# Loading and turning A for the first two regions of a 4096-cube matmul: pieces, order of issue and turns

## The chip, the cores and the metric

One core of one Trainium2 chip. The metric is device microseconds of one execution; the median of the fast runs is quoted (an execution can fall into a slower state of the chip). "Faster" or "slower" needs 2%, which is 36 us here.

## The reference

```
x = a @ b                                  # a, b: 4096 x 4096, fp32
out = where(x > 0, x, 0.01 * x)            # leaky ReLU, fp32
```

## The kernel before: the parts that matter

The product is cut into regions of 512 rows by 1024 columns: 4 row tiles (`MT`) times 2 column tiles (`NP`) of 128x512, which fill all eight PSUM banks. Chunks of k are 128 long; 32 chunks x 8 outputs = 256 matmuls to a region. Loads by POOL cast fp32 to bf16 on the way; A is then transposed on DVE.

The first two regions (the upper and the lower 512 rows, h = 0 and 1, of the same columns) share their B and are run interleaved, because loading is what is short at the start (in the kernel before, the windows view shows the DMA engines busy throughout from 5 to 140 us). The 32 chunks are cut into five segments, and a "turn" is a list of segments that are summed in PSUM for h = 0, then for h = 1. After each turn the sum is added to `part` in SBUF:

```
SEGS = [(0, 0, 4), (0, 4, 4), (1, 0, 8), (2, 0, 8), (3, 0, 8)]   # unit, first chunk, chunks
TURNS = [[0], [1], [2, 3, 4]]
...
def load_a(mb, h, s, mt, tiles):                 # loads and transposes in one
    ...
    a16 = a16_pool.tile([P, 4 * tiles, kw // 4], BF16, name="a16")
    for q in range(4):
        nc.gpsimd.dma_start(a16[32 * q:32 * q + 32], src.rearrange("(g i) w -> i g w", i=32))
    nc.vector.transpose(dst ..., a16 ...)
...
def spill(t, h, mt, banks):
    for nt in range(NP):
        kept = part[h][:, mt, nt * NT:(nt + 1) * NT]
        if t == 0: ...                            # ACT or DVE copies
        else:
            nc.vector.tensor_add(kept, banks[mt, nt], kept)
...
for quarter in range(4):                          # inside one step
    if last:
        todo = [(quarter, c) for c in range(kc)]
    else:
        todo = [(mt, quarter * kc // 4 + c) for c in range(kc // 4) for mt in range(MT)]
    ...                                           # matmuls of todo
    if last:
        spill(t, h, quarter, banks)
    quarter_of(following, quarter)                # a quarter of the next step's loads and transposes
```

A "step" is one segment for one h. Steps 0 to 3 have 32 matmuls each, steps 4 to 9 have 64.

## Time and profile before

| kernel before | us |
|---|---|
| time, median of 3 runs | 1792.63 |
| profiled span | 1790.5 |

The prediction below splits the span into the stream of real matmuls, the end of the kernel and the rest. The rest, the start of TensorE and its waits before 89 us, is about 20.6 us, and all a change of the start can win is part of it. The lines that show where it sits stand in the prediction. The word **lag** is used throughout as defined there: the time at which a matmul starts, less 0.2156 us for every real matmul before it. A wait raises it, nothing lowers it, and two kernels compare by their last lag.

### The profile page before, as it was taken

To read this page: it belongs to the slowest core of one execution; us is meant where nothing else is said; L and a number is where in the kernel's file an instruction comes from. 1 tells how busy PE (TensorE), PEld (TensorE's weight loads), DVE (VectorE), ACT (ScalarE), POOL (GpSimd) and SP (SyncE) were. 2 spreads that over 40 slices of the span, in tenths; PEclk is the share of its full clock that TensorE was granted. 3 is DMA by queue.
4 is the path that set the end of the run, shared out by engine and by line. 5 is a ranking of instruction groups with operands and counts; after the bars stand their busy time and mean duration, and the time that the engine had idled before them with its cause. 6 is when DMAs were issued, how large, how long until landed. Compare 5 with 4: busy or idle time off the path is not lost.

```text
span 1790.5 us, 18113 instructions
## 1 busy us (share of the span) xinstructions
PE 1775.6 (99%) x8220; PEld 803.6 (45%) x8220; DVE 141.9 (8%) x114; ACT 150.1 (8%) x266; POOL 369.0 (21%) x671
## 2 busy tenths in 40 slices
PE   8999999999999999999999999999999999999999
PEld 3444444444444444444444444444444444444444
DVE  5420000022100000002200000000220000000000
ACT  2000000000000000000000000000000000000001
POOL 5540110343002021043300202014320120201000
PEclk9999999999999999999999999999999999999999
DMA  9994661997229166398703917539860481835511
GB/s 214 215 230 94 127 144 58 190 122 128 66 71 193 53 112 135 85 187 129 129 37 94 188 47 118 117 95 201 129 116 24 106 176 48 160 75 119 117 48 47
DMA packets 163612, 212.49 MB, mean 119 GB/s; under 512 B 43600, under 2 KB 92752, under 8 KB 163536
## 3 DMA queue, kind: packets, MB, share of 16 engines
q0 software_dynamic: 143232, 141.08, 49.7%
q10 hardware_dynamic: 17856, 65.02, 9.3%
q1 hardware_dynamic: 2448, 5.24, 0.8%
q8 instruction: 64, 1.05, 0.2%
q14 instruction: 12, 0.10, 0.0%
HBM read 285.21 MB, written 67.11 MB: 197 GB/s over the span
## 4 chain that ended last, share of the span: by engine, by line
PE 95%; DMA 4%; POOL 0%; issue 0%; DVE 0%; ACT 0%; SPq 0%; DVEq 0%
PE ps L139 95%; DMA bt<-in_b_dram 2%; DMA a<-in_a_dram 1%; DMA a_in<-in_a_dram 0%; POOL a L113 0%; DVE at L114 0%; POOL bt L129 0%; ACT bt L247 0%; DVE part L216 0%; ACT o L336 0%; ACT at L254 0%; DVE a_rounded L249 0%; PE turned L252 0%; SPq L239 0%; SPq L237 0%
## 5 line engine op out<-in xcount | busy, mean ns | idle before, releaser
L139 PE MATMUL ps<-bt,at 128*128 128x512 bf16 x8192 | 1769.9, 379 | 9.2 <-DVE at L114 8.1
L139 PEld LDWEIGHTS <-at 128*128 128x128 bf16 x8192 | 801.0, 98 | 976.7 <-DVE at L114 10.0
L129 POOL DMA_DIRECT2D bt<-in_b_dram x412 | 219.7, 539 | 1099.7 <-PE ps L139 1042.0
L336 ACT ACTIVATE o<-ps 128x512 f32<-128x512 f32 x240 | 130.7, 595 | 1524.5 <-PE ps L139 1450.7
L114 DVE STREAM_TRANSPOSE at<-a 128x1024 uint32<-128x1024 uint32 x63 | 113.0, 1828 | 1165.9 <-DMA a<-in_a_dram 607.8
L113 POOL DMA_DIRECT2D a<-in_a_dram x252 | 148.5, 596 | 190.4 <-DVE at L114 125.4
L216 DVE TENSOR_TENSOR part<-ps,part 128x512 f32<-128x512 f32 x32 | 20.4, 682 | 30.9 <-PE ps L139 30.9
L219 ACT ACTIVATE o<-part 128x1024 f32<-128x1024 f32 x8 | 8.5, 1057 | 98.9 <-DVE part L216 86.8
L212 DVE COPY part<-ps 128x512 f32<-128x512 f32 x8 | 5.1, 672 | 1.7 <-PE ps L139 1.7
L214 ACT COPY part<-ps 128x512 f32<-128x512 f32 x8 | 4.4, 593 | 8.5 <-PE ps L139 5.3
L84 PE MATMUL ps<-w 128*128 128x512 bf16 x8 | 3.6, 628 | 1.2 <-DVE x L80 1.2
L247 ACT CAST bt<-b_in 128x1024 bf16<-128x1024 f32 (+1 forms) x4 | 3.8, 938 | 0.0
L252 PE MATMUL turned<-ident,a_rounded 128*128 128x128 bf16 x16 | 1.9, 246 | 0.8 <-DVE a_rounded L249 0.8
L252 PEld LDWEIGHTS <-a_rounded 128*128 128x128 bf16 x16 | 1.2, 123 | 2.7 <-DVE a_rounded L249 2.6
L84 PEld LDWEIGHTS <-w 128*128 128x128 bf16 x8 | 1.0, 138 | 2.9 <-issue 1.7
L254 ACT COPY at<-turned 128x256 bf16<-128x256 bf16 x4 | 1.8, 444 | 4.6 <-PE turned L252 4.6
L254 DVE COPY at<-turned 128x256 bf16<-128x256 bf16 x4 | 1.8, 448 | 4.4 <-ACT at L254 4.4
L249 DVE CAST a_rounded<-a_in 128x512 bf16<-128x512 f32 x4 | 1.7, 426 | 3.0 <-DMA a_in<-in_a_dram 2.7
L271 POOL CAST x<-bt 128x1 f32<-128x1 bf16 x1 | 0.2, 187 | 7.3 <-ACT bt L247 7.3
L81 ACT ACT_TABLE_LOAD x1 | 1.3, 1283 | 0.7 <-PEq L358 0.7
L267 PE MATMUL ps<-w 128*128 128x512 bf16 x4 | 1.3, 456 | 0.0
L267 PEld LDWEIGHTS <-w 128*128 128x128 bf16 x4 | 0.5, 135 | 0.4 <-issue 0.3
(10 smaller groups left out, 1.9 us busy)
## 6 DMA issues: line engine op xcount, KB each, us to landing
bt<-in_b_dram POOLq DMA_DIRECT2D x412, 256.0 KB, 7.6
out_dram<-o ACTq DMA_DIRECT2D x124, 512.0 KB, 3.3
a<-in_a_dram POOLq DMA_DIRECT2D x252, 128.0 KB, 5.6
out_dram<-o SPq DMA_DIRECT2D x8, 256.0 KB, 2.0
b_in<-in_b_dram SPq DMA_DIRECT2D x3, 512.0 KB, 5.4
a_in<-in_a_dram SPq DMA_DIRECT2D x4, 256.0 KB, 5.1
b_in<-in_b_dram SPq DMA_DIRECT2D x2, 256.0 KB, 6.6
```

Of the source, the lines that this page charges most:

```text
L84: nc.tensor.matmul(wp, w[:, :P], w, start=True, stop=True)
L113: nc.gpsimd.dma_start(a16[32 * q:32 * q + 32], src.rearrange("(g i) w -> i g w", i=32))
L114: nc.vector.transpose(dst.rearrange("p c m e -> p c (m e)").bitcast(U32) .rearrange("p c (g i) -> p g c i", g=4 * tiles), a16.rearrange("p ...
L129: nc.gpsimd.dma_start(new_b(pi, u)[:, c0 + c, :], b_rows(n, s, c))
L139: nc.tensor.matmul(ps, at[mb, h, u][:, c // 2, mt * P:(mt + 1) * P, c % 2], bt[pi, u][:, c, nt * NT:(nt + 1) * NT], start=first, stop=last,)
L212: nc.vector.tensor_copy(kept, banks[mt, nt])
L214: nc.scalar.copy(kept, banks[mt, nt])
L216: nc.vector.tensor_add(kept, banks[mt, nt], kept)
L219: nc.scalar.activation(o, part[h][:, mt, :], LRELU, alpha=alpha)
L247: copy(b0[:, i, columns(half)], b_in[:, i, columns(half)])
L254: copy(a0[:, c, i * P:(i + 1) * P, :].rearrange("p m e -> p e m"), turned[i][:, 2 * c:2 * c + 2, :],)
L336: nc.scalar.activation(o[:, cols], banks[mt, nt], LRELU, alpha=alpha)
```

## The change

Its intent: the first A of the lower half comes in two pieces so that work can start on the first; POOL's loads are released at the first B chunk instead of the second; a load and its transpose become two calls, so that all loads of the next step are issued at once at the beginning of a step, while the transposes are placed among the additions on DVE; and segments 2 and 3 are run for both halves before segment 4. The order of the very first loads changes too. (In the code, `fetch()` is the load and `turn()` the transpose; it has nothing to do with the turns of `TURNS`.)

```
-TURNS = [[0], [1], [2, 3, 4]]
+TURNS = [[0], [1], [2, 3], [4]]
...
+        def fetch(): ...        # the four DMAs
+        def turn(): ...         # the transpose
+        return fetch, turn
...
+        made = pieces_a(0, h, s, 2 if i == 1 else None) if i else []
...
-    order = []
-    for i in range(MT):
-        order += [("a", i, None)] + [("b", i, half) for half in ((0, 1) if i == MT - 1 else (None,))]
+    order = [("a", 0), ("a", 1), ("b", 0), ("a", 2), ("b", 1), ("a", 3), ("b", 2), ("b", 3)]
...
-        if (what, i) == ("b", 1):
-            nc.gpsimd.tensor_copy(x[:, :1], b0[:, 1, :1])      # POOL waits here before its first load
+        if (what, i) == ("b", 0):
+            nc.gpsimd.tensor_copy(x[:, :1], b0[:, 0, :1])
...
+        head = 0 if h else kc // 2 if last else kc
+        groups = [([(mt, c) for c in range(head) for mt in range(MT)], None)]
+        groups += [([(mt, c) for c in range(head, kc)], mt if last else None) for mt in range(MT)]
+        where = [2] if len(following) == 1 else [0, 3]         # (shortened)
...
+            for fetch in fetches[i + 1]:
+                fetch()
...
+            for piece, turn in enumerate(following):
+                if where[piece] == g:
+                    turn()
+            if leaves is not None:
+                spill(t, h, leaves, banks)
```

More of the change, by code (lines that the diff above doesn't have):

```diff
@@ L107, in load_a, with fetch, turn @@
         k0, kw = k_of(s)
-        dst = new_a(mb, h, u)[:, c0 // 2:(c0 + kc) // 2, mt * P:(mt + tiles) * P, :]
         row = ((mb * HALVES + h) * MT + mt) * P
-        a16 = a16_pool.tile([P, 4 * tiles, kw // 4], BF16, name="a16")
-        for q in range(4):
-            src = a[row:row + tiles * P, k0 + q * kw // 4:k0 + (q + 1) * kw // 4]
-            nc.gpsimd.dma_start(a16[32 * q:32 * q + 32], src.rearrange("(g i) w -> i g w", i=32))
-        nc.vector.transpose(
-            dst.rearrange("p c m e -> p c (m e)").bitcast(U32)
-            .rearrange("p c (g i) -> p g c i", g=4 * tiles),
-            a16.rearrange("p g w -> p (g w)").bitcast(U32)
-            .rearrange("p (g j c) -> p g c j", g=4 * tiles, c=kc // 2),
-        )
+        held = []
+        def fetch():
+            a16 = a16_pool.tile([P, 4 * tiles, kw // 4], BF16, name="a16")
+            for q in range(4):
+                src = a[row:row + tiles * P, k0 + q * kw // 4:k0 + (q + 1) * kw // 4]
+                to = a16[32 * q:32 * q + 32]
+                nc.gpsimd.dma_start(to, src.rearrange("(g i) w -> i g w", i=32))
+            held.append(a16)
+        def turn():
+            dst = new_a(mb, h, u)[:, c0 // 2:(c0 + kc) // 2, mt * P:(mt + tiles) * P, :]
+            nc.vector.transpose(
+                dst.rearrange("p c m e -> p c (m e)").bitcast(U32)
+                .rearrange("p c (g i) -> p g c i", g=4 * tiles),
+                held[0].rearrange("p g w -> p (g w)").bitcast(U32)
+                .rearrange("p (g j c) -> p g c j", g=4 * tiles, c=kc // 2),
+            )
+        return fetch, turn
     def b_rows(n, s, c):
@@ L129, in load_b, with pieces_a @@
         nc.gpsimd.dma_start(new_b(pi, u)[:, c0 + c, :], b_rows(n, s, c))
-    def pieces_a(mb, h, s):
-        tiles = 2 * KC // SEGS[s][2]
-        return [lambda mt=mt: load_a(mb, h, s, mt, tiles) for mt in range(0, MT, tiles)]
+    def pieces_a(mb, h, s, tiles=None):
+        tiles = tiles or 2 * KC // SEGS[s][2]
+        return [load_a(mb, h, s, mt, tiles) for mt in range(0, MT, tiles)]
     def pieces_b(pi, s):
@@ L181 @@
                     at_slot = first * KU + h * KU + u - 2 * KU + 1
-                    loads.setdefault(at_slot, []).extend(pieces_a(mb, h, s))
+                    for fetch, turn in pieces_a(mb, h, s):
+                        loads.setdefault(at_slot, []).extend([fetch, turn])
     def quarter_of(pieces, quarter):
@@ L194 @@
     ]
-    def step_loads(h, s):
-        made = pieces_a(0, h, s)
-        if h == 0:
-            own = pieces_b(0, s)
-            made = made[:1] + own[:4] + made[1:] + own[4:]
-        return made
-    queue = [step_loads(h, s) for _, h, s, _, _ in steps]
+    fetches = []
+    turns = []
+    for i, (_, h, s, _, _) in enumerate(steps):
+        made = pieces_a(0, h, s, 2 if i == 1 else None) if i else []
+        fetches.append([fetch for fetch, _ in made] + (pieces_b(0, s) if i and h == 0 else []))
+        turns.append([turn for _, turn in made])
     part = {}
@@ L227, with columns @@
     a_rounded = a16_pool.tile([P, MT, kw0], BF16, name="a_rounded", tag="a16")
-    order = []
-    for i in range(MT):
-        order += [("a", i, None)] + [("b", i, half) for half in ((0, 1) if i == MT - 1 else (None,))]
-    def columns(half):
-        return slice(0, RN) if half is None else slice(half * NT, (half + 1) * NT)
-    for what, i, half in order:
+    order = [("a", 0), ("a", 1), ("b", 0), ("a", 2), ("b", 1), ("a", 3), ("b", 2), ("b", 3)]
+    def columns(nt):
+        return slice(nt * NT, (nt + 1) * NT)
+    for what, i in order:
         if what == "a":
             nc.sync.dma_start(a_in[:, i, :], a[i * P:(i + 1) * P, :kw0])
-        else:
-            nc.sync.dma_start(b_in[:, i, columns(half)], b_rows(pairs[0], 0, i)[:, columns(half)])
+        elif i < kc0 - 1:
+            nc.sync.dma_start(b_in[:, i, :], b_rows(pairs[0], 0, i))
+        else:
+            for nt in range(NP):
+                nc.sync.dma_start(b_in[:, i, columns(nt)], b_rows(pairs[0], 0, i)[:, columns(nt)])
     a0 = new_a(0, 0, 0)
@@ L242, with take @@
     turned = [psum_pool.tile([P, kc0, P], BF16, name="turned", tag="ps") for _ in range(MT)]
-    def take(what, i, half):
+    def take(what, i):
         if what == "b":
-            copy = nc.vector.tensor_copy if half == 1 else nc.scalar.copy
-            copy(b0[:, i, columns(half)], b_in[:, i, columns(half)])
+            for nt, copy in ((0, nc.scalar.copy), (1, nc.vector.tensor_copy)):
+                copy(b0[:, i, columns(nt)], b_in[:, i, columns(nt)])
             return
@@ L259 @@
     there = {"a": [], "b": []}
-    ready = []
+    waiting = []
     begun = set()
     banks = {}
-    for n, (what, i, half) in enumerate(order):
-        take(what, i, half)
-        if n == 0:
+    for n, (what, i) in enumerate(order):
+        take(what, i)
+        if n == 1:
             for _ in range(4):
@@ L268 @@
             banks = new_banks()
-        if (what, i) == ("b", 1):
-            nc.gpsimd.tensor_copy(x[:, :1], b0[:, 1, :1])
+        if (what, i) == ("b", 0):
+            nc.gpsimd.tensor_copy(x[:, :1], b0[:, 0, :1])
             part[0] = part_pool.tile([P, MT, RN], FP32, name="part", tag="part")
-        if half != 1:
-            there[what].append(i)
-        if what == "a":
-            now = [(i, c, nt) for c in there["b"] for nt in range(NP)]
-        else:
-            now = [(mt, i, nt) for mt in there["a"] for nt in (range(NP) if half is None else (half,))]
-        ready.append(now)
-        for mt, c, nt in ready[n - 1] if n else []:
-            mm(banks[mt, nt], 0, 0, 0, 0, mt, nt, c, (mt, nt) not in begun,
-               what == "b" and half == 1 and c == kc0 - 1)
-            begun.add((mt, nt))
-    following = list(queue[1])
-    following.pop(0)()
-    for mt, c, nt in ready[-1]:
-        mm(banks[mt, nt], 0, 0, 0, 0, mt, nt, c, False, True)
+        for mt, c in waiting:
+            for nt in range(NP):
+                mm(banks[mt, nt], 0, 0, 0, 0, mt, nt, c, (mt, nt) not in begun, False)
+                begun.add((mt, nt))
+        there[what].append(i)
+        waiting = [(i, c) for c in there["b"]] if what == "a" else [(mt, i) for mt in there["a"]]
+    for fetch in fetches[1]:
+        fetch()
+    turns[1][0]()
+    for nt in range(NP):
+        for mt, c in waiting:
+            mm(banks[mt, nt], 0, 0, 0, 0, mt, nt, c, False, True)
+    for mt in range(MT):
         spill(0, 0, mt, banks)
-    for piece in following + queue[2]:
-        piece()
+    turns[1][1]()
+    for fetch in fetches[2]:
+        fetch()
     for i in range(1, len(steps)):
@@ L294 @@
         u, c0, kc = SEGS[s]
-        following = queue[i + 1] if 2 <= i and i + 1 < len(steps) else []
-        own = 2 * KU - 2 + i - (len(steps) - 2)
+        head = 0 if h else kc // 2 if last else kc
+        groups = [([(mt, c) for c in range(head) for mt in range(MT)], None)]
+        groups += [([(mt, c) for c in range(head, kc)], mt if last else None) for mt in range(MT)]
+        following = turns[i + 1] if i + 1 < len(steps) else []
+        if len(following) == 1:
+            where = [2]
+        else:
+            where = [0, 3]
+        own = 2 * KU - 2 + i - (len(steps) - 2)
+        own = list(loads.get(own, [])) if own >= 2 * KU - 2 else []
+        if i > 1 and i + 1 < len(steps):
+            for fetch in fetches[i + 1]:
+                fetch()
+        for piece in own:
+            piece()
         if first:
@@ L300 @@
                 part[h] = part_pool.tile([P, MT, RN], FP32, name="part", tag="part")
-        for quarter in range(4):
-            if last:
-                todo = [(quarter, c) for c in range(kc)]
-            else:
-                todo = [(mt, quarter * kc // 4 + c) for c in range(kc // 4) for mt in range(MT)]
+        for g, (todo, leaves) in enumerate(groups):
             for mt, c in todo:
@@ L309 @@
                        last and c == kc - 1)
-            if last:
-                spill(t, h, quarter, banks)
-            quarter_of(following, quarter)
-            if own >= 2 * KU - 2:
-                quarter_of(loads.get(own, []), quarter)
+            for piece, turn in enumerate(following):
[3 more added lines that the diff above has]
+                spill(t, h, leaves, banks)
     for r in range(HALVES, len(regions)):
```

## The prediction

> **What bounds the kernel now.** I read the page first, for which engine fills the span.
>
> ```profile
> PE 1775.6 (99%) x8220; PEld 803.6 (45%) x8220; DVE 141.9 (8%) x114; ACT 150.1 (8%) x266; POOL 369.0 (21%) x671
> ...
> PE   8999999999999999999999999999999999999999
> ```
>
> TensorE (PE) is busy nearly everywhere; only the first of the 40 slices (45 us each) is below 9. The windows view gives 1855 matmuls in each undisturbed 400 us, so one 128x512 matmul starts every 400/1855 = 0.2156 us, and the 8192 real ones need 8192 x 0.2156 = 1766.2 us. The profiled span is 1790.5. So only 24.3 us are not the matmul stream, and a change that removes no matmul can win at most those. The last matmul ends at about 1786.8 in the timeline, so 3.7 us are the last eviction and store, which the change does not touch. The rest is the start. I then asked who made PE wait in the whole trace.
>
> ```profile
> PE ps L139 <- DVE at L114: 8.1, 4, 2.4
> ...
> PE ps L139 <- DMA bt<-in_b_dram: 0.8, 1, 0.8
> PE ps L139 <- DVE part L216: 0.2, 1, 0.2
> ```
>
> The columns are total us, times, longest. Four waits for a transpose of A (L114) make up nearly all. PE's timeline says when they fall.
>
> ```profile
> 6.97 1.31 PE L139 MATMUL ps<-bt,at 128*128 128x512 bf16 x4
> ...
> 17.43 13.99 PE L139 MATMUL ps<-bt,at 128*128 128x512 bf16 x64 [2.07 <-DVE at L114]
> 33.81 7.95 PE L139 MATMUL ps<-bt,at 128*128 128x512 bf16 x36 [2.39 <-DVE at L114]
> 43.15 0.94 PE L139 MATMUL ps<-bt,at 128*128 128x512 bf16 x3 [1.40 <-DVE at L114]
> 44.31 29.30 PE L139 MATMUL ps<-bt,at 128*128 128x512 bf16 x135 [0.22 <-DVE part L216]
> 74.40 11.81 PE L139 MATMUL ps<-bt,at 128*128 128x512 bf16 x54 [0.79 <-DMA bt<-in_b_dram]
> 88.42 6.87 PE L139 MATMUL ps<-bt,at 128*128 128x512 bf16 x31 [2.20 <-DVE at L114]
> ```
>
> The reader is to see that nothing waits after 88.42. I keep one book, the **lag**: the time at which a matmul starts, less 0.2156 us for each real matmul before it. At 6.97 it is 7.0; at 17.43 (32 before it) 10.5; at 33.81 (96) 13.1; at 44.31 (135) 15.2; at 74.40 (270) 16.2; at 88.42 (324) 18.6. What the change makes of the time is what it makes of this last lag. VectorE (DVE) is 8% busy overall, but in the stretch before 44 us it is not idle at all where it matters.
>
> ```profile
> 31.31 1.29 DVE L216 TENSOR_TENSOR part<-ps,part 128x512 f32<-128x512 f32 x2 [0.44 <-PE ps L139]
> 32.52 1.23 DVE L114 STREAM_TRANSPOSE at<-a 128x1024 uint32<-128x1024 uint32 x1
> 35.60 1.29 DVE L216 TENSOR_TENSOR part<-ps,part 128x512 f32<-128x512 f32 x2 [1.85 <-PE ps L139]
> 36.81 2.02 DVE L114 STREAM_TRANSPOSE at<-a 128x1024 uint32<-128x1024 uint32 x1
> 38.75 2.44 DVE L216 TENSOR_TENSOR part<-ps,part 128x512 f32<-128x512 f32 x4
> 41.12 1.98 DVE L114 STREAM_TRANSPOSE at<-a 128x1024 uint32<-128x1024 uint32 x1
> 43.01 1.25 DVE L216 TENSOR_TENSOR part<-ps,part 128x512 f32<-128x512 f32 x2
> ```
>
> The transpose at 32.52 comes after all eight additions of the step before it, and PE, which had run dry at 31.4, starts at 33.81 when it is done. **This is an order of work on one engine, not missing data.**
>
> **What the Trainium skill says.** "TensorE: Matmul & The Clock Gate", Part 1 ("Wait — 56ns, not 53.3ns?"), gives 215.7 ns from start to start for a warm matmul of 512 columns; the trace agrees with 215.6. "PSUM — Partial Sum Buffer", "PSUM: the matmul accumulator", has eight banks, each of 512 fp32 columns, and one matmul output within one bank: a step of 4 x 2 outputs therefore fills all eight, and the next step enters a bank only once its sum is taken away. The trace shows that wait once (0.2 us, for L216). "Perfetto Trace Analysis", "Tensor Engine Instruction", calls DVE strict FIFO, so the program's order of additions and transposes is what runs; the DVE rows above stand in program order. "DMA: Bandwidth & Descriptors", "Anatomy of one DMA", fits 2.0 us + bytes/436e3, or 2.3 us as an estimate for 128 KB. The trace differs: 7.2 us median to landing for the A loads of the first 110 us, because up to eight are in flight at about 200 GB/s. The measurement decides.
>
> **The change part by part.** Steps: 0 and 1 are segment 0 of k (4 chunks, 32 matmuls, 6.9 us) for the upper and the lower half of rows; 2 and 3 the same for segment 1; then segments 2, 3, 4 (64 matmuls, 13.8 us each).
>
> *Step 0, reordered loads.* Now both A tiles come before the first B chunk, and each B chunk is rounded in halves on ACT and DVE. I worked the chain through with the trace's 0.43 (DVE rounding), 0.41 (PE transpose), 0.44 and 0.45 (ACT and DVE copies), about 0.6 and 0.45 (half chunks), and the landings it shows (first A 3.86, 1 MB by 6.2, then about 2.6 us a MB). The second A is rounded at 6.1, B chunk 0 on ACT 7.35 to 7.95, the third A from 8.2, first real matmuls at about 8.95 (before: 6.97), last A transposed at 11.2, and 26 matmuls after it: step 0 ends at about 16.75, against 15.36 before (10.88 + 4.48). Cost **+1.4**. "Loads begun at the first B chunk" moves POOL's first load from 8.75 to about 8.3 only.
>
> *Step 1, A in two pieces.* Before, four DMAs of 128 KB, issued 8.75 to 11.4, were transposed at 16.13 to 17.38. The first piece is now four of 64 KB, issued about 8.3 to 11, and should land near 14; its transpose takes half of 1.25, some 0.65 us. It is ready before 16.75, and banks are freed as step 1 needs them. The 2.07 us wait goes: step 1 starts at 16.75 instead of 17.43, lag 9.9 against 10.5. Second piece: transposed about 19, needed at 16.75 + 3.45 = 20.2.
>
> *Steps 2 to 4, transposes placed among the additions.* Step 2 starts at 23.65. It runs two chunks for all rows, then finishes row tile by row tile, so its first sum is ready after 20 matmuls at 27.95. From there I add up DVE in its new order. Before, from 26.13 to 44.26 is 18.13 us, of which 0.44 x 3 + 1.85 = 3.17 idle: 14.96 us for 16 additions and three transposes. The work is the same after. The new order is two additions, the transpose for step 3 (27.95 + 1.29 + 1.2 = 30.45, just when PE needs it at 30.55), six additions, transpose, four additions, transpose, four additions. It need not idle, so it ends at 27.95 + 14.96 = 42.9. Step 3 runs without a wait and ends at 37.45. But step 4 goes chunk by chunk over all four row tiles, and its eighth matmul needs the bank that the last of those additions frees. So the 2.39 wait goes and **a new one of about 4.5 us in total takes its place** at the start of step 4. Resume at 42.9 with 135 matmuls done: 42.9 - 29.1 = 13.8, against 15.2.
>
> *Four turns instead of three.* Segments 2 and 3 now run for both halves before segment 4. Before, the third 2 MB of B were needed from about 72 us (B wait at 74.40); now two 13.8 us steps that need only 1 MB of A come between, so loads at 200 GB/s get 27.6 us of slack. The 0.79 and the wait for a transpose queued late (2.20 at 88.42) should go, 3.4 us of lag from 15.2 to 18.6 with the small change. Added: 16 more additions, 16 x 0.65 = 10.4 us of DVE, in two steps of 13.8 us each, where the windows show DVE less than half busy; they lie beside PE.
>
> *Sum.* Final lag 13.8 against 18.6, or **-4.8 us**; by parts -0.6 by the start of step 1 (+1.4 and -2.07, rounded), -0.8 by step 4 (13.8 - 9.9 = 3.9 lost there, against 15.2 - 10.5 = 4.7) and -3.4 later. I allow 0.2 for a small new wait: 1792.6 - 4.6 = **1788.0 us**.
>
> **The rivals.** (1) DVE does not bind steps 3 and 4: if additions and transposes fit, the lag stays at 9.9 and the time is near 1784. Against: 14.96 us of DVE work in 9.5 us of PE time (27.95 to 37.45). (2) Loading is the bound: 64 KB DMAs cost POOL nearly the same issue time as larger ones (0.58 against 0.54 us for a different shape), eight instead of four come first, and segment 1's data arrive later; then the wait moves to step 2 and 2 to 4 us return, near 1791. For: the DMA share is over 1 from 10 us on. Against: 2.0 MB are due by 24 us and the rate before gave about 2.3. (3) Step 0 is worse than I have it, or PE's idle patches slow its clock: up to +2, near 1790; or its extra 1.4 us disappears in slack, near 1787. (4) The start is hidden by something later: no wait in the trace after 88.42 speaks for it, so what the start wins, the end keeps.
>
> **Range and chances.** The floor of all this is 1766.2 + 3.7 + about 9 of lag, and the 2.1 us by which the reported time exceeds the span, near 1781; returning to 1792 would need every gain spent in new waits. Eight in ten: 1785.8 to 1790.8. A change by 2% is 36 us, more than the whole start can give; only a blunder with all loads late would reach it upward. Faster 0.003, same 0.99, slower 0.007.
>
> **What would show it.** In the changed profile: first real matmul near 9, step 1 starting near 16.7 without a transpose wait; a wait of 4 to 5 us between 37 and 43 put down to additions (part) and a transpose, with DVE solid from 28 to 43; no wait for B near 74 and none near 88; steady 1855 matmuls per 400 us after. Wrong if step 2 waits for B, if step 0 ends after 18, if DVE has gaps at 28 to 43, or if a wait appears where segment 4 starts (about 97).

## The result

Median 1789.94 us in four runs (1787.88 to 1790.84) against 1793.04 in four of the kernel before. The ratio is 0.9981 (0.9963 to 0.9998). A ratio here is formed from the fast runs of both kernels in the same rounds, so it is not quite the ratio of the medians. The time was in the stated range, 1.9 us above the forecast; the forecast gain was 4.6 us, and the medians show 3.1.

PE's waits in the changed kernel (total us, times, longest):

```profile
PE ps L148 <- DVE part L225: 2.7, 4, 2.1
PE turned L262 <- DVE a_rounded L259: 1.6, 2, 1.3
PE ps L84 <- DVE x L80: 1.2, 1, 1.2
PE ps L148 <- DVE at L121: 0.9, 1, 0.9
```

L148, L225 and L121 are what L139, L216 and L114 were. The transposes, which held PE for 8.1 us, now hold it for 0.9; the additions have taken a part of their place, and the wait for B is gone. PE's timeline (start, duration, and in brackets the idle time before):

```profile
9.23 1.63 PE L148 MATMUL ps<-bt,at 128*128 128x512 bf16 x6
11.18 0.41 PE L262 MATMUL turned<-ident,a_rounded 128*128 128x128 bf16 x4 [0.32 <-DVE a_rounded L259]
11.43 19.59 PE L148 MATMUL ps<-bt,at 128*128 128x512 bf16 x90
31.93 8.25 PE L148 MATMUL ps<-bt,at 128*128 128x512 bf16 x36 [0.91 <-DVE at L121]
42.25 0.38 PE L148 MATMUL ps<-bt,at 128*128 128x512 bf16 x1 [2.07 <-DVE part L225]
...
44.04 86.27 PE L148 MATMUL ps<-bt,at 128*128 128x512 bf16 x392 [0.22 <-DVE part L225]
```

After 44.04 there is no wait at all. Step 1 follows step 0 without a gap (26 matmuls from 11.43 end near 17.0, then the next 64 go on). The lag at 44.04, with 135 matmuls done, is 44.04 - 29.1 = 14.9; the kernel before had 15.2 at the same matmul, and 18.6 at 88 us. By that book the gain should be 3.7 us, but the profiled spans differ by 2.1 only. The missing piece is in the windows view. Its columns are the stretch, its length, busy time and count for PE, weight loads, DVE, ACT and POOL, then granted clock, DMA share and GB/s:

```profile
40.00:43.00 3.00, 0.70 (x3) 0.29 (x3) 3.00 (x4) 0.00 (x0) 1.26 (x3) 1.00 1.13 209
43.00:44.00 1.00, 0.60 (x2) 0.10 (x1) 0.99 (x2) 0.00 (x0) 0.62 (x2) 0.85 1.08 203
44.00:47.40 3.40, 3.36 (x9) 1.23 (x9) 0.00 (x0) 0.00 (x0) 1.85 (x4) 0.54 1.32 193
47.40:50.00 2.60, 2.60 (x14) 1.18 (x12) 1.01 (x1) 0.00 (x0) 1.99 (x5) 1.00 1.45 194
```

From about 43.7 to 47.1 the granted clock is half: 9 matmuls start in 3.4 us where 16 or 17 should. The trace's clock record has one such window of 3.41 us there (43.71 to 47.12), which costs at most half of it, 1.7 us, and 1.5 if only the 3.1 us after 44.04 count. 14.9 + 1.7 = 16.6, and 18.6 - 16.6 = 2.0 (2.2 with the 1.5), close to the 2.1 between the spans. The stretch just before is the stall: DVE busy throughout and PE almost idle.

The additions and transposes on DVE, from the first addition to the last one that PE waits for:

```profile
28.32 1.29 DVE L225 TENSOR_TENSOR part<-ps,part 128x512 f32<-128x512 f32 x2 [3.48 <-PE ps L148]
30.63 1.25 DVE L121 STREAM_TRANSPOSE at<-a 128x1024 uint32<-128x1024 uint32 x1 [1.01 <-DMA a<-in_a_dram]
31.80 3.64 DVE L225 TENSOR_TENSOR part<-ps,part 128x512 f32<-128x512 f32 x6
35.36 2.01 DVE L121 STREAM_TRANSPOSE at<-a 128x1024 uint32<-128x1024 uint32 x1
37.30 2.45 DVE L225 TENSOR_TENSOR part<-ps,part 128x512 f32<-128x512 f32 x4
39.67 1.95 DVE L121 STREAM_TRANSPOSE at<-a 128x1024 uint32<-128x1024 uint32 x1
41.55 2.44 DVE L225 TENSOR_TENSOR part<-ps,part 128x512 f32<-128x512 f32 x4
```

From 30.63 to 43.99 DVE never idles, and PE resumes at 44.04. The one gap after the additions begin is new, and the prediction had named such a gap as a sign that it would be wrong: 1.01 us at 30.6, waiting for the A of step 3 to land.

### The profile page after: what moved, and what is told of

It reads as the page before. It is cut to its first block, busy times and chain, and to the rows that moved or that the text cites. A ratio compares the mean times of both kernels' runs of the same rounds, so it can differ in the third digit from the quotient of the medians.

```text
span 1788.4 us, 18154 instructions
## 1 busy us (share of the span) xinstructions
PE 1778.0 (99%) x8220; PEld 804.7 (45%) x8220; DVE 152.1 (9%) x134; ACT 148.8 (8%) x266; POOL 372.0 (21%) x675
## 4 chain that ended last, share of the span: by engine, by line
PE 98%; DMA 1%; DVE 0%; POOL 0%; ACT 0%; issue 0%; DVEq 0%
PE ps L148 98%; DMA a<-in_a_dram 1%; POOL a L116 0%; PE ps L84 0%; DVE at L121 0%; DVE part L225 0%; PE turned L262 0%; ACT at L264 0%; ACT o L356 0%; ACT bt L257 0%; DVE at L264 0%; DVE a_rounded L259 0%; POOL x L281 0%; DVE w L78 0%; DVEq L121 0%
## 5 line engine op out<-in xcount | busy, mean ns | idle before, releaser
L148 PE MATMUL ps<-bt,at 128*128 128x512 bf16 x8192 | 1771.1, 379 | 3.8 <-DVE part L225 2.7
L148 PEld LDWEIGHTS <-at 128*128 128x128 bf16 x8192 | 801.8, 98 | 972.2 <-issue 4.2
L121 DVE STREAM_TRANSPOSE at<-a 128x1024 uint32<-128x1024 uint32 (+1 forms) x64 | 113.1, 1800 | 1151.8 <-DMA a<-in_a_dram 593.8
L225 DVE TENSOR_TENSOR part<-ps,part 128x512 f32<-128x512 f32 x48 | 30.2, 679 | 31.5 <-PE ps L148 31.5
```

The costliest lines, as they stand in the source:

```text
L121: nc.vector.transpose(dst.rearrange("p c m e -> p c (m e)").bitcast(U32) .rearrange("p c (g i) -> p g c i", g=4 * tiles), held[0].rearrang ...
L148: nc.tensor.matmul(ps, at[mb, h, u][:, c // 2, mt * P:(mt + 1) * P, c % 2], bt[pi, u][:, c, nt * NT:(nt + 1) * NT], start=first, stop=last,)
```

## The experiments

Twelve runs, in three calls of four kernels. Each call ran on one chip, and each kernel was timed in five rounds beside the kernel before: medians of the latter 1792.41, 1793.30 and 1792.97 in calls 1, 2 and 3. All results were correct. In the experiments' profiles about 2% of the matmul records are missing (1818 of 1855 in 400 us, with all weight loads there), so a lag below counts the program's matmuls, not the records (x88 stands for 90).

### Call 1: the stall, the clock, and the two pieces

**after_again**: the changed kernel, no edit.

> The changed kernel once more, to count the clock. Its profile has a window of 3.41 us at half clock right after the stall of 39 to 44 us. Theory A (the stall brings the clock down): most runs show a mean clock of 0.999 and about 1790, and any run with 1.000 is some 2 us shorter. Rival B (the clock drop is an accident of its own): runs with 0.999 are as rare as in the kernel before, whose profiled run shows 1.000.

Measured: 1790.51, ratio 0.9985, mean clock of the profiled run 0.997. That profile has half clock in two places, at about 8.4 to 11.8 us in step 0, and from 42.5 us, as the stall ends, for two windows of 3.41 us. The record holds the mean clock of every run, and one such window takes about 0.001 off it. The changed kernel has 1.000 in one of its 14 runs (four in the result above, five here, five in after_b), and that run, 1787.88, is the shortest, 1.5 us below the next. This is what Theory A expected. But half clock is not rare in the kernel before either, as Rival B assumed: of its 27 runs, the 11 at 1.000 took 1791.44 to 1792.97, the five at 0.999 1792.01 to 1794.39, and the 11 at 0.998 1793.68 to 1794.78.

A mean of 1.000 does not say that step 0 ran at full speed. In the changed kernel's own profile the clock record begins only at 9.57 us, and four matmuls before that, at 6.96, took 1.91 us, against 1.03 in after_again.

**warm**: zeros are multiplied during the stall.

```
                 for nt in range(NP):
+                    if i == 4 and c == 0 and mt >= 2:
+                        for _ in range(8 if (mt, nt) == (2, 0) else 1):
+                            nc.tensor.matmul(banks[0, 0], w[:, :P], w, start=False, stop=False)
                     mm(banks[mt, nt], ...)
```

> The changed kernel with 11 matmuls of zero weights put into the stall at the start of the first 64-matmul step (they add 0 to a bank already begun). The additions that PE waits for stay as they are, so PE resumes the real work at about 44 as before. Theory A: PE no longer looks idle, the half-clock window goes, mean clock 1.000 in all runs, and the time is 1.7 us (3.41 us at half speed) below the changed kernel, about 1788.2. Rival B: the window stays, and the time is that of the changed kernel, 1789.9, or longer by what the added matmuls take.

Measured: 1788.10, ratio 0.9970, **2.4 us below the changed kernel in the same rounds**. PE was let into the last of the eight banks at 43.78, about as late as ever; the same windows of this run:

```profile
40.00:43.00 3.00, 2.60 (x12) 0.99 (x11) 3.00 (x4) 0.00 (x0) 1.45 (x3) 1.00 1.12 209
43.00:44.00 1.00, 0.99 (x5) 0.29 (x4) 0.73 (x2) 0.00 (x0) 0.55 (x2) 1.00 1.12 209
44.00:47.40 3.40, 3.40 (x17) 1.56 (x16) 0.00 (x0) 0.00 (x0) 1.83 (x5) 1.00 1.38 191
```

17 matmuls instead of 9, at clock 1.00. The profile still has the early half-clock window in step 0 (mean clock 0.999), so the expected "1.000" was too much, but the late one is gone. Extra matmuls that do nothing made the kernel faster. One profile would not settle it, but the mean clocks of the runs agree: by them warm's five runs lost 3 windows in all and after_again's five 9, an estimate of 6 x 1.7 / 5 = 2.0 us a run, most of the 2.4. Theory A holds: the stall, when PE is left idle in it, is what brings the late half clock (not every time: see call 3), and the half clock costs extra.

**pairs**: step 4 does the first four chunks for row tiles 0 and 1, then for 2 and 3, and only then the rest.

```
+        if first and not last and h == 0:
+            half = kc // 2
+            groups[0] = (
+                [(mt, c) for c in range(half) for mt in (0, 1)]
+                + [(mt, c) for mt in (2, 3) for c in range(half)]
+                + [(mt, c) for c in range(half, kc) for mt in range(MT)],
+                None,
+            )
```

> The changed kernel, where the first 64-matmul step runs chunks 0 to 3 of row tiles 0 and 1 first, then of tiles 2 and 3, then the rest. It first needs the banks of tiles 2 and 3 some 3.4 us later. Theory C (VectorE binds only because the step's eighth matmul needs the last addition): the stall of 39 to 44 shrinks from about 3.4 us idle to under 0.7, no half clock follows, lag at 50 us about 12 in place of 16.5, time about 1785. Rival D (the chunks of B land too late to be used faster, about one per 1.25 us until 46): the stall turns into waits for B of 2 to 3 us, time 1788 or more.

Measured: 1786.05, ratio 0.9958, 4.5 us below the changed kernel in the same rounds. PE's timeline:

```profile
11.77 19.59 PE L148 MATMUL ps<-bt,at 128*128 128x512 bf16 x88
32.44 87.73 PE L148 MATMUL ps<-bt,at 128*128 128x512 bf16 x394 [1.08 <-DVE at L121]
```

No stall and no half clock in this profile (1.000; the other four runs have 0.999), although DVE is as busy as before and makes its last addition of the stretch until 44.5. Theory C holds, Rival D falls: B was there. The same DVE work is harmless when the eight matmuls that open a step do not need all eight banks at once. The 4.5 us hold the clock's share as well as the stall's: by the mean clocks the five runs lost 5 windows fewer than after_again's, an estimate of 1.7 us a run. The lag is 32.44 - 96 x 0.2156 = 11.7.

**onepiece**: the lower half's first A is loaded whole.

```
-        made = pieces_a(0, h, s, 2 if i == 1 else None) if i else []
+        made = pieces_a(0, h, s) if i else []
...
-    turns[1][1]()
```

> The changed kernel with the lower half's first A loaded whole again (four DMAs of 128 KB in place of eight of 64 KB). Theory E (the halves cost POOL issue time, 4 x 0.62 = 2.5 us, and the step is not ready for the first piece anyway): the A of step 3, which landed 1.0 us late at 30.6, is there in time; the transpose for step 1 starts near 16 and ends near 17.3, at most 0.4 us late; net 0.5 to 1 us faster, 1789. Rival F (the halves carry the gain of the start): step 1 begins a full us later and the time rises to 1791.

Measured: 1789.79, ratio 0.9979, 0.7 us below the changed kernel in the same rounds, with half clock in both places. PE's timeline shows a wait of 0.40 for the transpose at step 1 (at 18.21) and none at step 3. Theory E holds in its mechanism; the size is not clear from run times here, since by the mean clocks these five runs lost 5 half-clock windows and after_again's 9, which alone could make the 0.7. POOL's rows, of the changed kernel and of the kernel before, say why:

```profile
8.41 7.48 POOL L116 DMA_DIRECT2D a<-in_a_dram  x12
8.75 5.25 POOL L113 DMA_DIRECT2D a<-in_a_dram  x8
```

In the changed kernel 12 DMAs from 8.41 on, eight of 64 KB and four of 128 KB, took 7.48 us, or 0.62 each, and in the kernel before eight of 128 KB from 8.75 on took 5.25, or 0.66 each. Half the bytes cost POOL nearly the same.

### Call 2: the turns, and two faster versions

**before_turns4**: the kernel before with one line changed.

```
-TURNS = [[0], [1], [2, 3, 4]]
+TURNS = [[0], [1], [2, 3], [4]]
```

> The kernel before with only its list of turns changed, from three to four. Theory G (the later gain is the turns alone): the waits of 0.79 at 74 and 2.20 at 88 us go, the stalls before 45 stay as they were (8.1 less 2.2), lag at 100 us near 15.3 in place of 18.6, time some 3.1 us below the kernel before, about 1789.4. Rival H (the old loads, issued a quarter of a step at a time, come too late for any order): a wait of 1 to 3 us returns where segment 4 starts, time 1791 or more.

Measured: 1792.58, ratio 0.9998 (0.9984 to 1.0011): no difference can be told. Theory G falls, but Rival H did not foresee the cause either. The wait for B is gone; the wait for a transpose is not, it only moved. PE and DVE of that run:

```profile
73.19 47.19 PE L139 MATMUL ps<-bt,at 128*128 128x512 bf16 x206 [2.20 <-DVE at L114]
```

```profile
69.94 1.29 DVE L216 TENSOR_TENSOR part<-ps,part 128x512 f32<-128x512 f32 x2 [2.17 <-PE ps L139]
71.15 5.77 DVE L114 STREAM_TRANSPOSE at<-a 128x1024 uint32<-128x1024 uint32 x3
```

The transpose that step 6 needs for its row tiles 2 and 3 stands behind the last additions of step 5 on DVE, as that for step 7 did at 86 us in the kernel before. And this 2.20 us wait too was followed by half clock, from about 73.8 to 77.2 us (0.50 in the stretch 74 to 77); its 1.7 us are more than the 0.79 of the missing wait for B. (At clock 1.000, its two runs took 1791.16 and 1791.65, and the four of the kernel before in this call 1791.81 to 1792.15: without half clock the missing wait may show, but not the 3.4 us.)

**after_turns3**: the changed kernel with three turns.

> The changed kernel with its list of turns put back to three. Theory G: waits for B or for a transpose of about 3 us return near 70 to 90 us, time 1793, no better than the kernel before. Rival H (the loads of a whole step issued at once have cured those waits by themselves): no wait after 45, time within 1 us of the changed kernel, 1790.

Measured: 1788.36, ratio 0.9975, and no wait after 44 us; PE's last row up to 120 us:

```profile
43.64 76.57 PE L148 MATMUL ps<-bt,at 128*128 128x512 bf16 x347 [0.22 <-DVE part L225]
```

So Rival H holds. The time was even below the changed kernel of earlier calls, but three of these five runs have a clock of 1.000, and it was another chip and other rounds.

**best1**: pairs and onepiece together, with the old order of the first loads and POOL released at the second B chunk.

```
-    order = [("a", 0), ("a", 1), ("b", 0), ("a", 2), ("b", 1), ("a", 3), ("b", 2), ("b", 3)]
+    order = [(what, i) for i in range(MT) for what in "ab"]
...
-        if n == 1:                               # the four warm-up matmuls
+        if n == 0:
...
-        if (what, i) == ("b", 0):
-            nc.gpsimd.tensor_copy(x[:, :1], b0[:, 0, :1])
+        if (what, i) == ("b", 1):
+            nc.gpsimd.tensor_copy(x[:, :1], b0[:, 1, :1])
```

> The changed kernel with the row-tile pairs, the lower half's A in one piece, and the old order of the first loads with POOL released at the second B chunk. The old order keeps PE busy between 5 and 7 us. If the early idle time is what brought the half clock at 8 to 12 us in three of five profiles, it is not there now. Step 1 is ready when A is, near 17.3; lag 10.5 to 10.9 from then on without any later wait; time about 1784.5. If the order of the start is of no account, 1785.7, as with the pairs alone.

Measured: 1783.86 (1783.84 to 1784.59), ratio 0.9950. Once step 0 runs there is one wait, 0.74 us for the transpose at step 1 (16.54). The clock is 1.000 in all five runs, as in the 15 runs of the three kernels built on this one: the early half clock of the new first order is gone, as expected. The old order was not put back alone, so its share of the gain is not shown.

**best2**: as best1, with POOL released at the first B chunk.

> As best1, with POOL released at the first B chunk, which in the old order is rounded at about 6.2 us. Theory I (step 1 waits for its A, so an earlier release pays): A transposed near 15.4, step 1 starts near 15.7, a wait of up to 1 us for the additions returns in the first 64-matmul step, lag 9.3, time about 1783.3. Rival J (the released loads take DMA time from the first step's own): step 0 ends 1 to 2 us later, time 1785.

Measured: 1783.66 (1783.47 to 1784.42), ratio 0.9949, the best and level with best1. PE's timeline:

```profile
11.62 4.48 PE L148 MATMUL ps<-bt,at 128*128 128x512 bf16 x19
16.28 103.91 PE L148 MATMUL ps<-bt,at 128*128 128x512 bf16 x470 [0.18 <-DVE at L121]
```

The transpose was ready by 16.2 in place of 15.4, and step 0 ended near 16.1, about 0.3 later than in best1 (the last first-step matmuls begin at 11.62 against 11.33). Theory I and Rival J may each have a part that nearly cancels, but this is not shown: the last first-step matmuls begin at 10.88 in the kernel before and at 11.23 in before_turns4, which start alike, so 0.3 us is within what one profile differs from another. The lag is 16.28 - 6.9 = 9.4, and no wait follows.

### Call 3: what the turns and the pieces are worth

**after_b**: the changed kernel, no edit.

> The changed kernel beside the one with three turns, on the same chip and in the same rounds. Expected near 1790.3, the median of its nine runs so far.

**turns3_b**: the changed kernel with three turns, in the same rounds.

> The changed kernel with three turns again. Theory K (the turns are worth nothing once loads and transposes are issued apart, and its 1788.4 was the clock): within 0.7 us of the changed kernel in the same rounds, and profiles with a half-clock window after the stall at 44 us lie near 1790, those without near 1788. Rival L (three turns are really better, because 16 additions fewer are made): 1.5 to 2 us below the changed kernel again.

Measured: 1789.62 and 1789.48, ratios 0.9982 and 0.9980. The difference is 0.1 us, so Rival L falls and Theory K holds in what it says of the turns: they are worth nothing here. What it says of the clock is half borne out: turns3_b, with half clock after the stall in its profile, took 1789.94 in that run; after_b had none after the stall, but one in step 0, and still took 1789.62. The same stall thus does not bring the clock down each time; after_turns3 had it without half clock too, so four of the six profiles with this stall show it. The traces say what may decide. Where the clock changes on record, it does so on a grid of 3.41 us that is not tied to the kernel's start. In the changed kernel one such window took in most of the stall; in after_b two windows shared it (the changed kernel first):

```profile
40.30:43.71 3.41, 1.02 (x3) 0.39 (x4) 3.41 (x5) 0.00 (x0) 1.54 (x3) 1.00 1.12 208
39.32:42.73 3.41, 1.60 (x7) 0.56 (x6) 3.41 (x5) 0.00 (x0) 1.50 (x3) 1.00 1.12 209
42.73:46.14 3.41, 2.33 (x9) 0.87 (x9) 2.15 (x4) 0.00 (x0) 1.73 (x3) 1.00 1.20 201
```

In the 14 profiles each of the nine falls to half clock on record (that after the last matmul left out) comes right after a window with PE busy 0.97 to 1.54 us, and none after the busier ones, of which the idlest have 1.56, 1.59 and 1.60. No experiment tested this, and a missing matmul record is worth about 0.2 us, so the border is not sharp. Why half clock lasted two windows in after_again stays open.

**best2_turns3**: best2 with three turns.

> best2 with three turns. PE reaches segment 4 at about 64.6 us there, some 6 us earlier than the changed kernel with three turns did. Theory M (the turns start to pay when PE runs ahead): waits for B or its transposes of 1 to 3 us return between 60 and 75, time 1784.7 to 1786.7. Rival N (loads keep up anyway): no wait, 1783.7 as best2.

Measured: 1784.17, ratio 0.9949, as best2 within the spread. Its profile has a wait of 0.22 for B at 65.13 and one of 0.45 for a transpose at 66.60, which best2 does not have. So by the trace the turns begin to pay when PE runs 5 us earlier, but 0.7 us and not 1 to 3; the run times do not show it.

**best2_halves**: best2 with the two pieces.

> best2 with the lower half's first A in two pieces, as the changed kernel has it. Theory E (halves cost 2.5 us of POOL issue and the A of step 3 lands late): step 1 starts at once near 16.1, but a wait of 0.5 to 1.5 us comes at step 3, lag 9.8 to 10.5, time 1784.2 to 1785. Rival (halves do no harm, and save best2's 0.2 us wait at step 1): 1783.5.

Measured: 1784.58, ratio 0.9953, against best2's 1783.66 on another chip. PE's timeline:

```profile
31.55 88.82 PE L148 MATMUL ps<-bt,at 128*128 128x512 bf16 x399 [1.39 <-DVE at L121]
```

The wait at step 1 is gone and a wait of 1.39 us stands at step 3; lag 31.55 - 20.7 = 10.9, against 9.4. Theory E holds again, a little above its range: the pieces move the wait to step 3 and make it longer.

Not tried: the fetches issued ahead without the new places of the transposes, and the reverse; nor the old order of the first loads alone. Which of the two removed the waits at 74 and 88 us is read from the traces only: the one at 88 was a transpose standing behind additions, the one at 74 a load.

## Why the prediction was right or wrong

- **Floor and bound**: right. Both kernels keep their 0.2156 us per matmul after the start (1855 in 400 us; the experiments show as many weight loads), and everything won or lost lies before 90 us.
- **Step 0, +1.4**: right in kind, short in size. First real matmul at 9.23 (forecast 8.95), end near 17.0 (16.75), against 15.2 before when counted in the same way (10.88 plus 20 matmuls), so 1.8 in place of 1.4; POOL's first load at 8.41 (8.3). With the old order back in best1 and best2, step 1 starts at 16.54 and 16.28 in place of 17.0, so 0.5 to 0.8 us of it was won.
- **Step 1 starts without a wait**: right, at 17.0.
- **Step 3's transpose "just when PE needs it"**: wrong by 0.9 us. The sum treated the loads as hidden; DVE's gap of 1.01 us at 30.6 is one of the signs by which the prediction said it would be wrong. Rival (2) named the extra POOL issues, but looked for the wait at step 2. It came at step 3, and onepiece and best2_halves tie it to the pieces.
- **The new wait at step 4**: right in place and cause, and in size by the lag. DVE had no gap after 30.63 and PE resumed at 44.04 (42.9 forecast; the first addition came 0.4 us later than forecast, the late A cost 1.0, and DVE's work took 0.3 less). The lag rose there from 31.93 - 20.7 = 11.2 to 14.9, by 3.7 us; the forecast lags were 9.9 and 13.8, or 3.9. The "about 4.5" of its text does not follow from its own sum, and the profile puts 2.7 us of waiting down to it, under the "4 to 5" it looked for. The experiment pairs removed the wait, and with it and its half clock 4.5 us.
- **"Steady" after the stall**: wrong, and the largest miss. The sum ended the stall at 42.9 and went on at full speed. The profile has 3.41 us at half clock, **1.5 to 1.7 us that no term of the sum held**. Rival (3) did name it, in the words "PE's idle patches slow its clock: up to +2, near 1790", without saying at which stall, and the median of 1789.94 is where that rival put it. The experiment warm shows that PE's idleness is the cause. The lag of 14.9 in place of 13.8 (1.1, mostly the late A) and the clock are together about the 2.7 us by which the profiled gain, 2.1, falls short of the forecast 4.8. The medians show 3.1 and not 2.1, and the clock explains that too: the profiled run of the kernel before had 1.000, but in the calls 16 of its 27 runs have less.
- **Four turns, -3.4**: right in size, wrong in cause. The waits after 45 did vanish. But turns alone gave nothing (before_turns4), and without them the waits vanish too (after_turns3, turns3_b): the transposes no longer stand behind the additions and the loads are issued a step ahead. This is the step whose reasoning failed; that the number came out was luck, because another part of the same change did the work.
- **Two readings**: the 2.1 us by which the reported time is said to exceed the span compares a median with another run's span; for the profiled run it is 1.8 (1792.31 and 1790.5), and the floor near 1781 moves by as much. And DVE is not "not idle at all" before 44 us: the prediction's own lines have gaps of 0.44 and 1.85.

What stays open: the kernel before has runs near 1792 and others near 1794.5 in all calls. The clocks on record tell them apart (medians 1792.06 for the 11 at 1.000, 1794.59 for the 11 at 0.998), so the longer runs are those with half clock. In which of its waits it falls is not shown, since its only profile is of a run at 1.000.

## What to carry to other kernels

Count for each engine which wait ends last before the next step may enter its banks, and if an in-order engine cannot finish in time, change the order in which the consumer asks, not only the order in which the producer delivers. A stall of TensorE can cost more than its own length, since the clock may stay at half for a further 3.4 us (6.8 in after_again); filling it with idle matmuls is a quick test of that. And test each part of a bundled change alone: here the turns did nothing and the two pieces cost time, while most of the gain, by elimination, came from issuing loads and transposes apart.

## What the Trainium skill lacked or had wrong

- "TensorE: Matmul & The Clock Gate", "HAM oscillation — how this bites in real kernels", gives as its rule that TensorE should have no idle gap above some 3.4 us (the section after it also tells of a clock lost to frequent short idles, without a figure). Here half clock followed stalls whose longest single gap was 2.07 us (three matmuls in the 3.9 us from 40.18 to 44.04) and a single gap of 2.20 us in before_turns4, and it appeared in step 0 in 4 of 8 profiles with the new first order, where the longest gap was 1.33. PE was still busy 0.97 to 1.54 us of the 3.41 us window before each fall. The same page's Part 1 says that the window is free-running and 3.4 us long; the record agrees (3.41 us, clock 0.50), and so does the chance in it: after_b and after_turns3 had the same stall and no half clock after it.
- The same page has nothing on filling a stall with matmuls that do no work: 11 of zero weights kept the clock at 1.00 there, and the time fell by 2.4 us.
- "DMA: Bandwidth & Descriptors", "Anatomy of one DMA — SWDGE (gpsimd) path", calls descriptor generation small and fits 2.0 us + bytes/436e3 to a DMA, 2.15 us for 64 KB as an estimate. Here POOL spent 0.62 us per issue when most DMAs were of 64 KB and 0.66 when all were of 128 KB, so issue hardly got cheaper with size; landing took 3.6 us (median of the eight of 64 KB) and 5.7 (128 KB, first 110 us).
